# Attention of a two-layer trunk: a pair's preparation in shorter VectorE steps, 1/rms from ScalarE's ln and exp with one Newton step, and transposes issued later

## The chip, the cores and the metric

The kernel runs as one program on one core of a Trainium2 chip. The metric is device time in microseconds (us), from runs of the whole program. The core's engines are TensorE (PE in the profile; PEld is its loading of weights), VectorE (DVE), ScalarE (ACT), GpSimd (POOL) and SyncE (SP, which issues DMAs). Each engine takes its own instructions in the order in which they were placed, and waits where an operand is not ready.

## The reference, cut to what matters

Two layers process 128 context tokens (the prompt) and 1024 latent tokens. Each layer projects its input, runs three groups of heads (attention, a short convolution, retention), joins them by `w_o`, and follows with a dense SwiGLU block. Attention has 8 heads; a query and a key have 96 numbers, of which the last 32 carry a rotary position code (rope). Both are divided by their own root mean square (rms) before the scores are made:

```python
q = (_rmsnorm(q_lat, q_norm_g) @ w_q_up).reshape(b, t, MLA_HEADS, QK_HEAD)
q = _rmsnorm(q, q_head_g)
k, v = _mla_kv(c_kv, k_pe, w_kv_up, k_head_g)
if latent:
    q = jnp.concatenate([q[..., :QK_NOPE], _rope_2d(q[..., QK_NOPE:])], axis=-1)
    k = jnp.concatenate([k[..., :QK_NOPE], _rope_2d(k[..., QK_NOPE:])], axis=-1)
    k_c, v_c = _mla_kv(ctx_ckv, ctx_kpe, w_kv_up, k_head_g)
    k = jnp.concatenate([k, k_c], axis=1)
    v = jnp.concatenate([v, v_c], axis=1)
attn = _attention(q.transpose(0, 2, 1, 3), k.transpose(0, 2, 1, 3), v.transpose(0, 2, 1, 3))
```

`_rmsnorm` is `x * rsqrt(mean(x * x) + EPS)`, and `_attention` a softmax of `q k / sqrt(96)` times `v`. The latent queries meet 1024 latent and 128 cached context keys, 9 key tiles of 128. The prompt's 128 tokens attend only to themselves.

## The kernel before

A layer runs in four stages: `in_proj` (projections of the layer's input, with the convolution, retention and the first pair's preparation placed between them), `attention`, the output projection, and the SwiGLU block. The change touches `in_proj` in one number, and `attention`. Products that must be exact to float32 are split in a high and a low part, so one product is three matmuls.

`attention(l, R, x)` works on 8 heads in 4 pairs. It is written as Python generators whose `yield`s mark where work may be broken off:

- `head_main` (the main work of one head): for each of 9 key tiles, three matmuls for each half of the 1024 queries (lines 1127 to 1129) into one of three PSUM tiles called mm, ScalarE's exponential of each (line 1130), and the product of the tile before with v (line 1110, tile ax, 64 rows of output). GpSimd adds the exponentials up over key tiles (lines 1113 and 1119), since their sum divides the result at the end.
- `head_prep` (through `heads`; one head ahead): transposes of the pair's k and q (line 1070), copies to high and low parts (ScalarE, line 1073; VectorE, line 1074), then 24 products for the scores' row maxima (line 1081), each reduced by VectorE (line 1083). The last reduction and a sign change give `mn` (lines 1087, 1088), which TensorE transposes (line 1090) and VectorE spreads over 8 extra rows of q (line 1092), so that the main products come out with the maximum subtracted.
- `pair_prep` (through `pairs`; one pair ahead): 10 token tiles, each with 9 matmuls (lines 960 to 969) or 3 for the last, ScalarE's copies and sums of squares (`ssq`, lines 971 to 981), one `yield` per tile. Then VectorE's chain: three operations on `ssq`, `rsq` for 1/rms (line 233: a bit trick in two operations, and three Newton steps of three operations each, lines 239 to 241, in tiles `rsy` and `rst`), and per half of the tokens `rope` (lines 918 to 921, products `rp`) and the products of q and k with 1/rms (lines 995, 997, 998).
- `pairs` then lets `GAP` (5) yields pass, marks the pair ready, and runs `prompt`: the prompt's own small attention of that pair (lines 1016 to 1050). After the last pair it loads and splits parts of the next stage's input (`mix_load`).

`attention` runs `head_main` of head h, and after each of its yields advances the other two by credit: `acc[0]` gains `RA` (1.3) for `heads`, whose yields carry prices (`CT`, `CM`, `CB`), and `acc[1]` gains `RB` (0.7) for `pairs`, one step per whole unit. What is left of the heads' credit goes to the pairs at `RX`. `LEAD` says from which yield on the next head may be prepared. A scheduler then orders the instructions of each engine by this order and their dependencies. All small products (transposes, maxima, projections, the products with v) share five PSUM tiles called `ax`. The first pair's `pair_prep` runs inside `in_proj`, advanced by `step(3)` after each column block.

## Time and profile before

| what | value |
|---|---|
| median of 3 runs | 3169.8 us (3165.72 to 3171.39) |
| profiled execution, its own time | 3169.16 us |
| its span, first to last instruction | 3167.4 us |
| mean granted TensorE clock | 0.977 of full speed |
| busy share of TensorE, VectorE, ScalarE, GpSimd | 96%, 56%, 35%, 37% |

The profiled execution is one run with the hardware profiler on. Its span leaves out what lies before the first and behind the last instruction. The busy shares are means over all four stages of both layers; attention, which the change touches, takes the stretch from about 380 to 700 us in layer 0 and from about 1943 to 2263 us in layer 1, a fifth of the span together. A window's row gives the busy time of each engine in it, with the count of instructions in brackets, and the granted clock in shares of the full one.

### The profile page before, as it was taken

The numbers are of one execution on the slowest core, as the hardware profiler recorded it, in microseconds if no ns is written. First come the engines' busy times: TensorE is split into PE (matmuls) and PEld (weight loads), VectorE is DVE, ScalarE is ACT, GpSimd is POOL, SyncE is SP. The second block draws the span as 40 slices with busy tenths as digits, with TensorE's granted clock in tenths as the row PEclk, the third lists the DMA queues.
The fourth block names the chain that finished last, engine by engine and source line by source line (L and its number), as shares of the span: only waits on it lengthen the run. The fifth ranks groups of instructions, "written<-read, shape, count | busy, mean of one in ns | idle before, by whom it ended". The sixth has DMA issues, their size and how long they took to land.

```text
span 3167.4 us, 48782 instructions
## 1 busy us (share of the span) xinstructions
PE 3033.0 (96%) x19136; PEld 2686.3 (85%) x19136; DVE 1778.7 (56%) x3483; ACT 1113.2 (35%) x2646; POOL 1178.4 (37%) x764
## 2 busy tenths in 40 slices
PE   6999999999799999999999999899988999999999
PEld 5988855459799999998999896554788999999999
DVE  6264476766954555633272646767588455556343
ACT  4333455444522222321153235454444222223211
POOL 3111243465643443411242103434656434343212
PEclk8999998999899999999999999999998999999999
DMA  5323000123222122576231110010322222226323
GB/s 211 103 95 128 22 12 1 60 91 107 83 81 74 63 84 81 178 251 237 66 113 48 49 32 13 12 53 8 121 100 69 84 84 71 69 71 220 101 67 100
DMA packets 126726, 278.06 MB, mean 88 GB/s; under 512 B 24097, under 2 KB 47393, under 8 KB 126497
## 3 DMA queue, kind: packets, MB, share of 16 engines
q1 hardware_dynamic: 126496, 274.95, 25.8%
q8 instruction: 151, 2.47, 0.3%
q14 instruction: 79, 0.64, 0.1%
HBM read 222.57 MB, written 52.33 MB: 87 GB/s over the span
## 4 chain that ended last, share of the span: by engine, by line
PE 81%; DVE 12%; DMA 2%; ACT 2%; issue 2%; POOL 1%; SPq 0%; DVEq 0%; POOLq 0%; ACTq 0%
PE mm L227 14%; PE mm L229 14%; PE mm L228 14%; PE ax L227 6%; PE ax L229 6%; PE ax L228 6%; PE ax L1110 5%; PE ax L1081 2%; PE mm L1127 2%; PE mm L1129 2%; PE mm L1128 1%; PE ax L325 1%; PE ax L1070 1%; DVE mx L1083 1%; POOL W L213 1%
## 5 line engine op out<-in xcount | busy, mean ns | idle before, releaser
L213 POOL TENSOR_TENSOR W<-r,W 128x512 fp32r<-128x512 f32 x336 | 447.8, 1346 | 541.7 <-ACT W L212 530.7
L213 POOL TENSOR_TENSOR W<-W,W 128x640 fp32r<-128x640 f32 (+5 forms) x168 | 298.4, 1777 | 827.9 <-ACT W L212 477.1
L227 PE MATMUL mm<-gh,W 128*128 128x384 f32 x1056 | 354.8, 336 | 1.9 <-DVE u L1401 1.1
L229 PE MATMUL mm<-gh,W 128*128 128x384 f32 x1056 | 353.3, 335 | 0.9 <-POOL W L213 0.8
L228 PE MATMUL mm<-gl,W 128*128 128x384 f32 x1056 | 352.9, 334 | 0.0
L1246 DVE SCALAR_TENSOR_TENSOR x<-mm,mod,x 128x128 f32<-128x128 f32 (+2 forms) x320 | 157.9, 515 | 329.7 <-PE mm L229 327.6
L229 PE MATMUL ax<-hth,W 128*128 128x288 f32 x1056 | 314.6, 298 | 10.1 <-POOL W L213 10.1
L227 PE MATMUL ax<-hth,W 128*128 128x288 f32 x1056 | 314.8, 298 | 7.6 <-ACT W L212 7.6
L228 PE MATMUL ax<-htl,W 128*128 128x288 f32 x1056 | 314.1, 298 | 0.0
L1119 POOL TENSOR_TENSOR W<-W,W 128x1024 f32<-128x1024 f32 x96 | 230.8, 2404 | 222.2 <-ACT W L1130 220.6
L212 ACT CAST W<-r 128x512 fp32r<-128x512 f32 x336 | 205.2, 621 | 184.8 <-DMA r<-in_w_up 63.8
L212 ACT CAST W<-W 128x640 fp32r<-128x640 f32 (+5 forms) x168 | 131.5, 783 | 390.6 <-DMA W<-in_w_down 178.7
L1083 DVE TENSOR_REDUCE mx<-ax 128x1 f32<-128x384 f32 x384 | 195.7, 550 | 115.2 <-PE ax L1081 112.8
L1130 ACT ACTIVATE W<-mm 128x512 f32<-128x512 f32 x288 | 168.5, 605 | 218.1 <-PE mm L1129 210.6
L227 PE MATMUL mm<-hh,W 128*128 128x384 f32 x704 | 240.5, 342 | 0.0
L229 PE MATMUL mm<-hh,W 128*128 128x384 f32 x704 | 239.0, 339 | 0.0
L228 PE MATMUL mm<-hl,W 128*128 128x384 f32 x704 | 237.9, 338 | 0.0
L1110 PE MATMUL ax<-W,vt 128*64 128x512 f32 x576 | 208.4, 658 | 8.2 <-DVE attn L1162 6.7
L229 PEld LDWEIGHTS ax<-hth,W 128*128 128x128 f32 x1056 | 201.2, 191 | 11.3 <-POOL W L213 11.3
L227 PEld LDWEIGHTS mm<-gh,W 128*128 128x128 f32 x1056 | 198.2, 188 | 13.0 <-issue 9.9
L227 PEld LDWEIGHTS ax<-hth,W 128*128 128x128 f32 x1056 | 201.4, 191 | 8.5 <-ACT W L212 8.5
L228 PEld LDWEIGHTS ax<-htl,W 128*128 128x128 f32 x1056 | 201.3, 191 | 0.0
(333 smaller groups left out, 7864.7 us busy)
## 6 DMA issues: line engine op xcount, KB each, us to landing
W<-in_ada_w SPq DMA_DIRECT2D x80, 512.0 KB, 5.1
gr<-gd SPq DMA_DIRECT2D x44, 576.0 KB, 5.4
r<-in_w_gate SPq DMA_DIRECT2D x96, 256.0 KB, 2.8
r<-in_w_up SPq DMA_DIRECT2D x96, 256.0 KB, 4.2
W<-in_w_in_fm SPq DMA_DIRECT2D x30, 512.0 KB, 3.7
W<-in_w_down SPq DMA_DIRECT2D x48, 320.0 KB, 3.5
gd<-gu SPq DMA_DIRECT2D x22, 576.0 KB, 3.7
gd<-gu SPq DMA_DIRECT2D x44, 224.0 KB, 2.2
```

The costliest lines, as they stand in the source:

```text
L212: self.nc.scalar.copy(hi, raw)
L213: self.nc.gpsimd.tensor_tensor(lo, raw, hi.bitcast(F32), op=ALU.subtract)
L227: self.nc.tensor.matmul(ps, wh, xh, start=first and i == 0, stop=False)
L228: self.nc.tensor.matmul(ps, wh, xl, start=False, stop=False)
L229: self.nc.tensor.matmul(ps, wl, xh, start=False, stop=last and i == n - 1)
L1081: nc.tensor.matmul(ps, qh[0:96, qt * P:(qt + 1) * P], kh[0:96, c * CH:(c + 1) * CH], start=True, stop=True)
L1083: nc.vector.reduce_max(mx[:, qt, c:c + 1], ps, axis=AX.X)
L1110: nc.tensor.matmul(po[64 * qc:64 * qc + 64, :], vv[:, kt, b:b + 64], prs[kt][:, qs], start=(kt == 0), stop=(kt == 8))
L1119: nc.gpsimd.tensor_tensor(acc, acc, prs[kt], op=ALU.add)
L1127: nc.tensor.matmul(ps, kh[0:104, ks], qh[0:104, qs], start=True, stop=False)
L1130: nc.scalar.activation(pr[:, qs], ps, AF.Exp, scale=SCALE)
L1246: self.nc.vector.scalar_tensor_tensor(x[m][:, t0:t1], ps[:, t0 - c * CH:t1 - c * CH], self.mod[l][:, j, m, i:i + 1], x[m][:, t0:t1], ALU.m ...
```

## The change

1. `1/rms`: `rsq` is replaced by ScalarE's `Ln` and `Exp` (with scale -0.5) and one Newton step of three VectorE operations.
2. `rope_steps` is `rope` with a yield behind each two operations, and further yields stand in VectorE's chain. `RB` rises from 0.7 to 1.0, and `GAP` with its five yields becomes two.
3. In `prompt`, the scaling of q, k, the maxima and the probabilities goes from VectorE to ScalarE, and the product with `gq` to GpSimd. Three yields are added.
4. In `head_prep` the reduction for `mn` gives the negated maximum itself, and a second yield of price `CB` stands between it and the transpose.
5. In `in_proj`, from the tenth column block on the background work advances by four steps instead of three.

```diff
@@ -48,7 +48,7 @@
 
 
 CT, CM, CB, RX = 0.7, 1.4, 0.7, 0.5
-RA, RB, LEAD, GAP = 1.3, 0.7, 14, 5
+RA, RB, LEAD = 1.3, 1.0, 14
 
 
 def segs(c):
@@ -780,7 +780,7 @@
                 else:
                     nc.scalar.copy(dst[:, cs], ps)
                 self.tick(ticks)
-                step(3)
+                step(4 if i > 8 else 3)
             if kind == "rq":
                 rq.append(dst)
             elif kind == "gc":
@@ -919,6 +919,18 @@
         nc.vector.tensor_tensor(t2, x, tab[:, 1].unsqueeze(2).to_broadcast(sh), op=ALU.mult)
         nc.vector.tensor_tensor(out[:, :, :, 0:16], t1[:, :, :, 0:16], t2[:, :, :, 16:32], op=ALU.subtract)
         nc.vector.tensor_tensor(out[:, :, :, 16:32], t2[:, :, :, 0:16], t1[:, :, :, 16:32], op=ALU.add)
+
+    def rope_steps(self, x, tab):
+
+        V = self.nc.vector
+        sh = [P, 4, x.shape[2], 32]
+        t1, t2 = self.Tt("rp1", sh), self.Tt("rp2", sh)
+        V.tensor_tensor(t1, x, tab[:, 0].unsqueeze(2).to_broadcast(sh), op=ALU.mult)
+        V.tensor_tensor(t2, x, tab[:, 1].unsqueeze(2).to_broadcast(sh), op=ALU.mult)
+        yield
+        V.tensor_tensor(x[:, :, :, 0:16], t1[:, :, :, 0:16], t2[:, :, :, 16:32], op=ALU.subtract)
+        V.tensor_tensor(x[:, :, :, 16:32], t2[:, :, :, 0:16], t1[:, :, :, 16:32], op=ALU.add)
+        yield
 
     def pair_weights(self, l, p, R):
         if ("w", p) not in R:
@@ -980,21 +992,31 @@
             for j in range(2):
                 nc.scalar.activation(sq[:, j, 0:64], kvp[:, j * 64:(j + 1) * 64], AF.Square, accum_out=ssq[:, 2 + j, t:t + 1])
             yield
-        V = nc.vector
+        V, G = nc.vector, nc.gpsimd
         V.tensor_tensor(ssq[:, 2:4, :], ssq[:, 2:4, :], R["kvs2"].unsqueeze(1).to_broadcast([P, 2, 10]), op=ALU.mult)
         V.tensor_tensor(ssq[:, 2:4, :], ssq[:, 2:4, :], R["kpss"].unsqueeze(1).to_broadcast([P, 2, 10]), op=ALU.add)
+        yield
         V.tensor_scalar(ssq[:, 2:4, :], ssq[:, 2:4, :], 1.0 / 96, EPS, ALU.mult, ALU.add)
         V.scalar_tensor_tensor(ssq[:, 0:2, 0:9], ssq[:, 0:2, 0:9], 1.0 / 96,
                                R["qms"].unsqueeze(1).to_broadcast([P, 2, 9]), ALU.mult, ALU.add)
-        r = self.rsq(ssq, (P, 4, 10))
+        r, t = self.sm("rsy", (P, 4, 10)), self.sm("rst", (P, 4, 10))
+        nc.scalar.activation(r, ssq, AF.Ln)
+        nc.scalar.activation(r, r, AF.Exp, scale=-0.5)
+        yield
+
+        V.tensor_tensor(t, r, r, op=ALU.mult)
+        V.scalar_tensor_tensor(t, t, -0.5, ssq, ALU.mult, ALU.mult)
+        yield
+        V.scalar_tensor_tensor(r, t, 1.5, r, ALU.add, ALU.mult)
         yield
         for b in range(2):
-            self.rope(q[b][:, :, :, 64:96], R["rtab"][:, :, 4 * b:4 * b + 4])
+            yield from self.rope_steps(q[b][:, :, :, 64:96], R["rtab"][:, :, 4 * b:4 * b + 4])
             t0, n = 1 + 4 * b, 4 + b
             bc = lambda i, n, m: r[:, i:i + 2, t0:t0 + n].rearrange("p a b -> p b a").unsqueeze(3).to_broadcast([P, n, 2, m])
             V.tensor_tensor(q[b], q[b], bc(0, 4, 96), op=ALU.mult)
             yield
             V.tensor_tensor(k[b][:, :, :, 0:64], k[b][:, :, :, 0:64], bc(2, n, 64), op=ALU.mult)
+            yield
             V.tensor_tensor(k[b][:, :, :, 64:96],
                             R["kper"][:, t0:t0 + n, :].unsqueeze(2).to_broadcast([P, n, 2, 32]), bc(2, n, 32), op=ALU.mult)
             yield
@@ -1013,10 +1035,13 @@
         at = self.attn_tile(p, R)
         gains = self.gains(l)
         for hh in range(2):
-            V.tensor_tensor(pr[:, hh, 64:96], pr[:, hh, 64:96], R["gq"], op=ALU.mult)
-            V.tensor_scalar(pr[:, hh, :], pr[:, hh, :], r[:, hh, 0:1], None, ALU.mult)
-            V.tensor_scalar(pr[:, 2 + hh, 0:64], pr[:, 2 + hh, 0:64], r[:, 2 + hh, 0:1], None, ALU.mult)
-            V.tensor_scalar(pr[:, 2 + hh, 64:96], R["kper"][:, 0, :], r[:, 2 + hh, 0:1], None, ALU.mult)
+            nc.gpsimd.tensor_tensor(pr[:, hh, 64:96], pr[:, hh, 64:96], R["gq"], op=ALU.mult)
+            nc.scalar.mul(pr[:, 2 + hh, 0:64], pr[:, 2 + hh, 0:64], r[:, 2 + hh, 0:1])
+            nc.scalar.mul(pr[:, 2 + hh, 64:96], R["kper"][:, 0, :], r[:, 2 + hh, 0:1])
+        yield
+        for hh in range(2):
+            nc.scalar.mul(pr[:, hh, :], pr[:, hh, :], r[:, hh, 0:1])
+        yield
         pt = self.ax((96, 4, P))
         for i in range(4):
             nc.tensor.transpose(pt[:, i, :], pr[:, i, :], self.ident)
@@ -1029,14 +1054,15 @@
             nc.tensor.matmul(ps[:, hh, :], qk[:, hh, :], qk[:, 2 + hh, :], start=True, stop=True)
         m, den = self.sm("pm", (P, 2)), self.sm("pden", (P, 2))
         V.reduce_max(m, ps, axis=AX.X)
-        V.tensor_scalar(m, m, -SCALE, None, ALU.mult)
+        nc.scalar.mul(m, m, -SCALE)
         pp = self.Tt("pp", (P, 2, P))
         for hh in range(2):
             nc.scalar.activation(pp[:, hh, :], ps[:, hh, :], AF.Exp, scale=SCALE, bias=m[:, hh:hh + 1],
                                  accum_out=den[:, hh:hh + 1])
         V.reciprocal(den, den)
         for hh in range(2):
-            V.tensor_scalar(pp[:, hh, :], pp[:, hh, :], den[:, hh:hh + 1], None, ALU.mult)
+            nc.scalar.mul(pp[:, hh, :], pp[:, hh, :], den[:, hh:hh + 1])
+        yield
         yield
         pt = self.ax((P, 2, P))
         for hh in range(2):
@@ -1082,10 +1108,10 @@
                                  start=True, stop=True)
                 nc.vector.reduce_max(mx[:, qt, c:c + 1], ps, axis=AX.X)
                 yield CM / 3
+        mn = self.sm("mn", (P, 8))
+        nc.vector.tensor_reduce(mn, mx, axis=AX.X, op=ALU.max, negate=True)
         yield CB
-        mn = self.sm("mn", (P, 8))
-        nc.vector.reduce_max(mn, mx, axis=AX.X)
-        nc.vector.tensor_scalar(mn, mn, -1.0, None, ALU.mult)
+        yield CB
         pt = self.ax((8, P))
         nc.tensor.transpose(pt, mn, self.ident)
         o, _ = VEC["eye8"]
@@ -1181,10 +1207,9 @@
                 yield from self.pair_prep(l, p, R)
                 if p < 3:
                     self.pair_weights(l, p + 1, R)
-                for _ in range(GAP):
-                    yield
+                yield
+                yield
                 R["ready", p] = True
-                yield
                 yield from self.prompt(l, p, R)
             while self.head_lim < 7:
                 yield
```

The places where the order changes most lie around pairs 1 and 2 of layer 0. On VectorE, at the end of head 3's maxima, the rows before read as follows (`mx` are the maxima by block, `mn` the negated row maximum, `rp` the rope products, `qt` and `kt` the pair's q and k, `rsy` 1/rms, `W` the head's q with its 8 extra rows):

```order
L1083 TENSOR_REDUCE mx_4293<-ax_4489 128x1
L918 TENSOR_TENSOR rp_787_4492<-qt_3990,rtabq_2373 128x256
L919 TENSOR_TENSOR rp_788_4493<-qt_3990,rtabq_2373 128x256
L1087 TENSOR_REDUCE mn_4502<-mx_4293 128x8
L997 TENSOR_TENSOR kt_3992<-kt_3992,rsy_4409 128x10x64
L920 TENSOR_TENSOR qt_3990<-rp_787_4492,rp_788_4493 128x8x16
L921 TENSOR_TENSOR qt_3990<-rp_788_4493,rp_787_4492 128x8x16
L1088 TENSOR_SCALAR mn_4502<-mn_4502 128x8
L998 TENSOR_TENSOR kt_3992<-kper_2354,rsy_4409 128x10x32
L995 TENSOR_TENSOR qt_3990<-qt_3990,rsy_4409 128x768
L1092 TENSOR_TENSOR W_4181<-ax_4505,vec_95 8x1024
```

In the changed kernel the same place reads:

```order
L1109 TENSOR_REDUCE mx_4327<-ax_4471 128x1
L928 TENSOR_TENSOR rp_788_4476<-qt_3976,rtabq_2373 128x256
L1112 TENSOR_REDUCE mn_4474<-mx_4327 128x8
L929 TENSOR_TENSOR rp_789_4477<-qt_3976,rtabq_2373 128x256
L1018 TENSOR_TENSOR kt_3978<-kt_3978,rsy_4339 128x10x64
L1118 TENSOR_TENSOR W_4224<-ax_4491,vec_95 8x1024
L931 TENSOR_TENSOR qt_3976<-rp_788_4476,rp_789_4477 128x8x16
L932 TENSOR_TENSOR qt_3976<-rp_789_4477,rp_788_4476 128x8x16
L1020 TENSOR_TENSOR kt_3978<-kper_2354,rsy_4339 128x10x32
L1016 TENSOR_TENSOR qt_3976<-qt_3976,rsy_4339 128x768
```

The sign change of line 1088 is gone, `mn`'s reduction has moved ahead of one rope product, and its use (the product on 8 partitions, line 1092 before and 1118 after) stands ahead of the rest of the rope. The last product on `kt` still follows behind four more operations.

On TensorE, the last projection of pair 1 (`cch` and `ccl` are the cached context's latents, `kTh` and `kTl` the head's k, `vt` its v) stands before in this order; from its last row there are 30 rows to the first transpose of that pair's k:

```order
L1127 MATMUL mm_3716<-W_2784,kTh_2782 128x512
L1128 MATMUL mm_3716<-W_2785,kTh_2782 128x512
L1129 MATMUL mm_3716<-W_2784,kTl_2783 128x512
L967 MATMUL ax_3721<-qwh_3325,cch_2343 128x256
L968 MATMUL ax_3721<-qwl_3326,cch_2343 128x256
L969 MATMUL ax_3721<-qwh_3325,ccl_2344 128x256
L1110 MATMUL ax_3329<-W_3654,vt_2421 64x512 x2
```

In the changed kernel it stands between a head's maxima (line 1107), and 48 rows lie between its last row and the first transpose of the pair's k:

```order
L1107 MATMUL ax_3668<-kTh_3335,W_3337 128x384
L1136 MATMUL ax_3322<-W_3586,vt_2421 64x512
L979 MATMUL ax_3671<-qwh_3318,cch_2343 128x256
L980 MATMUL ax_3671<-qwl_3319,cch_2343 128x256
L981 MATMUL ax_3671<-qwh_3318,ccl_2344 128x256
L1136 MATMUL ax_3322<-W_3586,vt_2421 64x512
L1107 MATMUL ax_3683<-kTh_3335,W_3337 128x384
```

The projection has moved ahead against the main work of the head, and the transposes have kept their place.

On ScalarE, behind the last sums of squares of pair 1 (`sqj`, `ssq`), the order before is (line 1130 are the exponentials):

```order
L981 ACTIVATE sqj_3727,ssq_3387<-ax_3721 128x64 x2
L1130 ACTIVATE W_3750<-mm_3751 128x512
L1130 ACTIVATE W_3750<-mm_3756 128x512
L1130 ACTIVATE W_3788<-mm_3789 128x512
L1130 ACTIVATE W_3788<-mm_3794 128x512
L1157 ACTIVATE dy_3802<-ax_3799 128x512
```

In the changed kernel the logarithm, the exponential for 1/rms and the scalings stand among those exponentials:

```order
L993 ACTIVATE sqj_3677,ssq_3358<-ax_3671 128x64 x2
L1156 ACTIVATE W_3694<-mm_3695 128x512
L1156 ACTIVATE W_3694<-mm_3700 128x512
L1003 ACTIVATE rsy_3709<-ssq_3358 128x40
L1004 ACTIVATE rsy_3709<-rsy_3709 128x40
L1156 ACTIVATE W_3721<-mm_3722 128x512
L1156 ACTIVATE W_3721<-mm_3727 128x512
L1039 ACTIVATE qt_3353<-qt_3353,rsy_3709 128x64
L1040 ACTIVATE qt_3353<-kper_2354,rsy_3709 128x32
L1039 ACTIVATE qt_3353<-qt_3353,rsy_3709 128x64
L1040 ACTIVATE qt_3353<-kper_2354,rsy_3709 128x32
```

Two exponentials stand between `Exp` of line 1004 and the first scaling of line 1039. Line 1003 needs VectorE's work on `ssq`, and line 1039 VectorE's Newton step.

## Rows read from the trace of the kernel before

**Rows 1.** The page: its first line, and busy time of each engine.

```profile
span 3167.4 us, 48782 instructions
...
PE 3033.0 (96%) x19136; PEld 2686.3 (85%) x19136; DVE 1778.7 (56%) x3483; ACT 1113.2 (35%) x2646; POOL 1178.4 (37%) x764
```

**Rows 2.** Windows of layer 0's attention: us, busy of PE, PEld, DVE, ACT, POOL, PEclk, DMA, GB/s.

```profile
380.00:700.00 320.00, 296.16 (x1261) 166.84 (x1260) 228.80 (x398) 160.34 (x502) 152.71 (x76) 0.95 0.10 37
```

**Rows 3.** The same view, seven short windows of that stage.

```profile
404.00:414.00 10.00, 5.95 (x22) 3.51 (x21) 9.95 (x12) 3.12 (x5) 6.88 (x4) 0.72 0.01 2
454.00:463.00 9.00, 6.70 (x31) 5.14 (x30) 6.89 (x9) 3.70 (x16) 2.37 (x1) 0.81 0.17 67
472.00:480.00 8.00, 6.23 (x17) 2.64 (x16) 8.00 (x21) 1.19 (x2) 4.14 (x2) 0.79 0.00 1
486.00:497.00 11.00, 7.30 (x27) 3.18 (x23) 9.04 (x10) 3.24 (x6) 7.13 (x5) 0.69 0.00 0
505.00:518.00 13.00, 10.63 (x31) 4.42 (x30) 10.29 (x16) 3.62 (x11) 6.38 (x3) 0.74 0.00 0
557.00:566.00 9.00, 5.58 (x19) 2.42 (x18) 8.85 (x12) 1.79 (x3) 4.71 (x3) 0.81 0.28 87
640.00:651.00 11.00, 7.75 (x19) 2.79 (x20) 9.76 (x15) 2.30 (x6) 5.28 (x3) 0.84 0.00 0
```

**Rows 4.** The same view, the last of these places in layer 1.

```profile
2203.00:2218.00 15.00, 11.76 (x23) 4.13 (x24) 11.19 (x18) 2.23 (x6) 6.10 (x3) 0.66 0.00 1
```

**Rows 5.** Order of time on DVE, 394 to 409: start us, us, operation, [idle before].

```profile
394.57 1.61 DVE L984 TENSOR_TENSOR ssq<-ssq,kvs 128x20 f32<-128x20 f32 x1 [1.46 <-ACT sqj L981]
...
397.89 0.28 DVE L921 TENSOR_TENSOR qt<-rp,rp 128x128 f32<-128x128 f32 x1
...
406.27 2.62 DVE L998 TENSOR_TENSOR kt<-kper,rsy 128x320 f32<-128x320 f32 x1
```

**Rows 6.** Order of time on DVE and POOL, 472 to 492.

```profile
472.45 1.91 DVE L237 TENSOR_SCALAR rsy<-rsy 128x40 int32<-128x40 int32 x1
...
484.00 2.92 DVE L997 TENSOR_TENSOR kt<-kt,rsy 128x640 f32<-128x640 f32 x1
...
488.30 2.39 POOL L1119 TENSOR_TENSOR W<-W,W 128x1024 f32<-128x1024 f32 x1
...
488.41 2.42 DVE L921 TENSOR_TENSOR qt<-rp,rp 128x128 f32<-128x128 f32 x1
...
490.76 1.07 DVE L1088 TENSOR_SCALAR mn<-mn 128x8 f32<-128x8 f32 x1
```

**Rows 7.** Order of time on DVE, 556 to 562.

```profile
556.94 2.40 DVE L240 SCALAR_TENSOR_TENSOR rst<-rst,ssq 128x40 f32<-128x40 f32 x1
...
560.08 1.80 DVE L241 SCALAR_TENSOR_TENSOR rsy<-rst,rsy 128x40 f32<-128x40 f32 x1
```

**Rows 8.** Order of time on DVE, 572 to 575.

```profile
572.31 2.66 DVE L998 TENSOR_TENSOR kt<-kper,rsy 128x320 f32<-128x320 f32 x1
```

**Rows 9.** Windows of tile rst: us, DVE busy (x), PEclk, DMA, GB/s.

```profile
380.00:700.00 320.00, 10.71 (x27) 0.95 0.10 37
```

**Rows 10.** Groups of line and form, 380 to 700: busy, mean ns | idle before.

```profile
L1088 DVE TENSOR_SCALAR mn<-mn 128x8 f32<-128x8 f32 x7 | 4.7, 673 | 0.2
...
L1019 DVE TENSOR_SCALAR qt<-kper,rsy 128x32 f32<-128x32 f32 x6 | 3.6, 594 | 0.0
...
L1017 DVE TENSOR_SCALAR qt<-qt,rsy 128x96 f32<-128x96 f32 x6 | 3.1, 509 | 0.0
...
L1032 DVE TENSOR_SCALAR pm<-pm 128x2 f32<-128x2 f32 x3 | 2.8, 925 | 0.0
...
L237 DVE TENSOR_SCALAR rsy<-rsy 128x40 int32<-128x40 int32 x3 | 2.2, 750 | 0.0
...
L1035 ACT ACTIVATE pp<-ax,pm 128x128 f32<-128x128 f32 x6 | 2.1, 362 | 4.1 <-DVE pm L1032 4.1
```

**Rows 11.** Waits of ACT, 380 to 700: us in total, times, longest us.

```profile
ACT pp L1035 <- DVE pm L1032: 4.1, 3, 2.9
```

## Prediction

> **What bounds the kernel now.** I read the page first: the span, the busy shares and the sliced busy digits. TensorE is busy 96% of the span [rows 1], so only the few stretches where it waits, or runs at half clock, can give time back; every engine that the change touches is far from full. The second view is the windows of the attention stage, where the edited code runs: of 320 us in layer 0, TensorE is busy 296.2, VectorE 228.8, ScalarE 160.3, GpSimd 152.7, and the granted clock is 0.95 [rows 2]. So 24 us are idle there, and more is lost to the clock. Layer 1 repeats the stage about 1563 us later.
>
> The third view is the same table cut around the seven places with idle of over 1.7 us [rows 3]. I call them A (404 to 414), B (454 to 463), C (472 to 480), D (486 to 497), E (505 to 518), F (557 to 566) and G (640 to 651). The idle is the width minus TensorE's busy time; the clock's loss I take as width times (1 minus the granted clock), an upper bound, since some of the slow clock falls into the idle itself. Each place is followed by a drop of the clock from 2.4 to 1.2 GHz. Idle plus clock: A 4.05 + 2.80, B 2.30 + 1.71, C 1.77 + 1.68, D 3.70 + 3.41, E 2.37 + 3.38, F 3.42 + 1.71, G 3.25 + 1.76; 37.3 us. In layer 1 they repeat; only G costs clearly more there, 3.24 + 5.10 [rows 4]. I take 37 us a layer for the rest of the working.
>
> What ends these waits is VectorE, which is busy 9.95 of the 10 us at A and all 8 at C [rows 3], although each of its operations there is small. Why it is late is seen in the order of time. The rope difference of line 921 takes 0.28 us at 397.89 [rows 5] and 2.42 us at 488.41; a GpSimd sum started at 488.30 and ended at 490.69, and the VectorE operation ended with it [rows 6]. Operations on PSUM, such as the maxima of line 1083, don't show this. Two or three such blocked operations in a row make a wait at TensorE: at C line 237 is 1.91 us long; at D lines 997 and 921 stand between the reduction for mn and its sign change (line 1088), which ends at 491.83, and TensorE's transpose waits for that [rows 6]. At F two of the Newton operations (2.40 and 1.80 us) stand ahead of the two attn products that release PSUM [rows 7]. A single blocked one does no harm: line 998 takes 2.66 us at 572.31 [rows 8], and no window with idle lies there, because five PSUM tiles are in flight.
>
> One page says the same and something that speaks against the change. The Trainium skill (SBUF — State Buffer, section Who interferes with whom) states that a VectorE instruction with two SBUF inputs contends with a GpSimd instruction that reads SBUF, and the loser waits for the whole instruction, while TensorE and ScalarE wait for nobody. The trace agrees (line 921: 0.28 against 2.42 us). By that rule what goes to ScalarE is free of the wait, but the two-input operations that stay are exposed as before, and spreading them out gives each its own chance to meet a GpSimd sum. What that would cost is the second rival below.
>
> **What the change removes.** Per pair eight of the eleven VectorE operations for 1/rms, the eight scalings and gain products of the prompt's q and k, the scaling of the prompt's maxima and of its probabilities; per head the sign change of line 1088. Over pairs 1 to 3 of a layer: Newton operations 10.7 us for 27 [rows 9], of which two thirds, 7.1 us; line 237 2.2, line 1017 3.1, line 1019 3.6, line 1032 2.8, line 1088 4.7 [rows 10]: 23.5 us, and some small ones not shown. That is a tenth of VectorE's busy time, and more than half of it is blocked time. It counts only at the places.
>
> **What it adds.** On ScalarE eleven small operations a pair; the nearest row, an exponential of 128 columns, takes 0.36 us [rows 10], so at most 4 us a pair or 12 us a layer on an engine that is idle for half of the stage. On GpSimd two products of 32 columns a pair, small beside sums of 2.4 us [rows 6]. More important, ScalarE now waits twice a pair for VectorE (ln for the sums of squares, the first scaling for the finished Newton step), and behind it in its queue stand the exponentials that empty TensorE's three mm tiles.
>
> **What it moves.** A pair's projections advance one step per half key tile instead of 0.7. In the order of TensorE pair 1's last projection is followed by 48 rows, not 30, before the first transposes of its k. At the stage's mean of 296.2 us for 1261 matmuls [rows 2], 0.235 us each, that is 4.2 us more lead (estimate). The reduction for mn now gives the sign itself, and a second short yield stands ahead of its transpose.
>
> **Place by place, in each layer.**
> - A, worth 6.9. VectorE's chain for pair 1 runs from 394.57 to 408.89, 14.3 us [rows 5]. It starts 4.2 earlier and loses (10.71 x 2/3 + 2.2) / 3 = 3.1 us of 1/rms operations, but takes in head 1's mn (0.7, the mean of line 1088 [rows 10]), the product on 8 partitions behind it, one more rope product, and ln and exp on ScalarE (0.36 each [rows 10]): some 3 us, with two estimates of 0.8 for the products. It ends about 4.3 us earlier, and the idle is 4.05. I take 5.
> - C, worth 3.5: line 237 is gone and the rest stands singly between maxima. I take 2.5.
> - D, worth 7.1: mn no longer waits behind lines 997, 920 and 921, but k's last product still stands behind all of them and the 8x1024 product, and the transposes of k come right after mn's; most of the wait moves there. I take 2.5. The bounds are 0 and 7.1.
> - E, worth 5.8: line 1032 and the two products on pp leave, the blocked reciprocal step stays. I take 3.
> - F, worth 5.1: the Newton operations are gone from between the attn products. I take 4.
> - B, worth 4.0, gets two rope products and one small operation on two inputs: some 1.0 us alone, up to 2.4 more if blocked. I take 1.5 as a loss.
> - G is the splitting of mix tiles, untouched.
> - ScalarE's new waits: bounds 0 and, per wait, the 2.9 us of the longest wait of ScalarE for VectorE now [rows 11]. TensorE has three mm tiles of cover. I take 1 us a pair, 3 a layer.
>
> 17 - 1.5 - 3 = 12.5 us a layer, 25 for both. In in_proj, pair 0's work is issued faster (four steps instead of three from the tenth weight on) and lies beside dense projections; I cost it at nothing, since a stall of a microsecond or two there is the most that so small a shift makes. The profiled execution took 3169.16 us, 1.8 more than its span and 0.6 less than the median of the runs, so 3169.2 - 25 = **3144 us**.
>
> **The rivals.**
> 1. Nearly everything goes: the five places A, C to F are worth 28.3 us a layer, less B's 1.5: 54 us, 3115. For it speaks that VectorE is the only releaser; against it, that D's chain keeps its length.
> 2. The waits form again: GpSimd is busy 0.48 of the stage [rows 2], so an isolated two-input operation meets a sum of 2.4 us about every second time and waits 1.2 us. Blocks that now come in a row come one by one, but twelve of them a pair leave room for two close ones. If one such pair of blocks costs what C costs now, 3.5 us, six pairs lose 21 of the 25 us: 3165, no change that can be told. The row at 572.31 speaks against it, the full windows of A and C for it.
> 3. ScalarE's queue, slower: the sums of squares or the Newton step are late by one or two blocks, ln or the scaling holds the exponentials, the three mm tiles run full and TensorE stops. If both waits cost 2.9 us, and each brings F's clock loss of 1.7, a pair loses 9.2, six lose 55, against 31 us gained without any: 24 us slower, 3193. It decides from 31 / 6 = 5.2 us a pair on. For it speaks that ScalarE already waits 4.1 us for VectorE in three times [rows 11]; against it, that between ln and the scaling two exponentials are placed, and that the three tiles hold some 2 us of TensorE's work.
>
> **How the numbers follow.** Forecast (3126 to 3155): 0.55. Rival 1 (under 3126): 0.08. Rival 2 and what lies between (3155 to 3176): 0.23, of which 0.10 is still below 3163.5. Rival 3 (over 3176): 0.14. About 0.2% (6.3 us) is what a measurement of this kernel tells from no change, so faster is under 3163.5: 0.73; within 0.13; slower 0.14. The range, 3116 to 3172, reaches to rival 1 and over rival 2; the forecast's own is 3126 to 3155.
>
> **What would show it.** At A the wait of the transposes for line 998's successor gone or under 1.5 us; no wait of mn's transpose behind k's product at D, but one of the transposes; F under 1 us; VectorE some 20 us less busy in the stage; the granted clock there up from 0.95 to about 0.97; G unchanged. It is wrong if TensorE waits for the exponentials, with ScalarE waiting for ssq or rsy for over 2 us at a time, or if the maxima are waited for at new places as long as at C.

## The result, and the profile after

The changed kernel takes 3117.94 us (median of 4 runs, 3115.68 to 3125.01), the kernel before 3169.74 us. The ratio is 0.9845, with a 95% interval of 0.9828 to 0.9863: 51.8 us faster. That is inside the stated range and on the forecast side, but it is twice the forecast gain of 25 us: the forecast's own band, 3126 to 3155, is missed, and the time lies where the first rival ("nearly everything goes", 3115) put it.

The page of the changed kernel, first line and busy times (to compare with [rows 1]):

```profile
span 3113.8 us, 48728 instructions
...
PE 3016.3 (97%) x19136; PEld 2678.3 (86%) x19136; DVE 1708.1 (55%) x3315; ACT 1131.7 (36%) x2734; POOL 1185.4 (38%) x780
```

The span is 53.6 us shorter. VectorE has 168 instructions fewer and 70.6 us less to do, ScalarE 88 more and 18.5 us more, which hardly move their shares.

To compare the stage I take it from its first main matmul to its last product with v. Before, it runs from 357.1 to 693.1 us in layer 0 and takes 335.9 us (338.5 in layer 1); after, from 353.7 to 665.9, 312.2 us (312.7). So 23.7 and 25.8 us of the 53.6 are gained in the two attention stages. The stretch up to layer 0's attention became 3.4 us shorter, but it varies from 351.7 to 357.2 over all traces of this study, among kernels that share its code too, so it is no effect that can be told.

The windows of the changed kernel's attention in layer 0, and of three short places in it (us, busy of PE, PEld, DVE, ACT, POOL, PEclk, DMA share, GB/s; to compare with [rows 2, 3]):

```profile
353.70:665.90 312.20, 304.84 (x1338) 173.59 (x1337) 206.67 (x352) 181.06 (x597) 160.00 (x83) 0.99 0.11 38
477.00:483.00 6.00, 4.83 (x28) 2.72 (x28) 5.97 (x8) 2.58 (x6) 3.97 (x4) 1.00 0.00 0
523.00:530.00 7.00, 5.32 (x27) 2.72 (x26) 6.26 (x12) 5.41 (x15) 2.63 (x3) 1.00 0.00 0
612.00:620.00 8.00, 4.34 (x12) 1.05 (x8) 7.97 (x10) 2.15 (x6) 4.36 (x2) 0.92 0.00 0
```

TensorE is idle for 7.4 of the 312.2 us, and the granted clock is 0.99 (0.95 before). The waits of TensorE in this stretch, all of them (engine, tile and line, releaser: us in total, times, longest):

```profile
PE ax L1107 <- DVE mx L1109: 3.6, 1, 3.6
PE ax L1096 <- DVE kTl L1100: 1.5, 1, 1.5
PE ax L1096 <- DVE kt L1020: 1.2, 1, 1.2
PE ax L1179 <- DVE W L1143: 0.5, 1, 0.5
PE ax L1179 <- POOL W L1143: 0.4, 1, 0.4
PE ax L1107 <- ACT W L1099: 0.2, 1, 0.2
```

Before, seven places had idle of over 1.7 us [rows 3]. One of them is left: the first row, which is G. The waits of A, B, C, E and F have no successor. D's has one, the third row: the transposes of k wait 1.2 us for k's last product (477 to 483), and the clock stays at 1.00 there. The second row is new, 1.5 us at 523 to 530, where VectorE's operations on the next pair, one of them held for 2.35 us at 521.91, stand ahead of the low parts of k (line 1100) that the transposes of q wait for; the clock stays full there too.

At A, the chain of pair 1, in order of time on DVE and POOL:

```profile
387.75 0.17 DVE L996 TENSOR_TENSOR ssq<-ssq,kvs 128x20 f32<-128x20 f32 x1
...
390.56 0.92 DVE L1007 TENSOR_TENSOR rst<-rsy 128x40 f32<-128x40 f32 x1
...
392.02 2.64 POOL L1145 TENSOR_TENSOR W<-W,W 128x1024 f32<-128x1024 f32 x1
...
392.36 3.12 DVE L1016 TENSOR_TENSOR qt<-qt,rsy 128x768 f32<-128x768 f32 x1
...
400.05 0.48 DVE L1020 TENSOR_TENSOR kt<-kper,rsy 128x320 f32<-128x320 f32 x1
```

It starts at 387.75, 34.1 us after the stage's start (394.57, 37.5 us, before [rows 5]), and ends at 400.53, 46.8 us after it (51.8 before). Three of its operations are still held by GpSimd sums: line 1007 takes 0.92 us, line 1016 takes 3.12, and line 1018 behind it 1.77 at 395.41. But TensorE does not reach the transposes of k until 404.81, so nobody waits.

At D, on DVE:

```profile
473.56 0.17 DVE L1112 TENSOR_REDUCE mn<-mx 128x8 f32<-128x24 f32 x1
...
477.24 1.35 DVE L932 TENSOR_TENSOR qt<-rp,rp 128x128 f32<-128x128 f32 x1
...
478.52 1.83 DVE L1020 TENSOR_TENSOR kt<-kper,rsy 128x320 f32<-128x320 f32 x1
```

`mn` is reduced at 473.6, ahead of the rope; two blocked operations (1.35 and 1.83 us) still stand ahead of k's transposes, where three did before (lines 997, 920 and 921 [rows 6]).

G, on DVE and POOL, is as it was: four splitting operations of `mix_split` take 6.1 us beside two GpSimd sums, and the maxima behind them come 3.6 us late. The first row is that of the kernel before.

```profile
639.17 5.76 DVE L1230 TENSOR_TENSOR mh<-mr,mh 128x288 fp32r<-128x288 f32 x4
...
611.04 6.08 DVE L1255 TENSOR_TENSOR mh<-mr,mh 128x288 fp32r<-128x288 f32 x4
...
611.45 4.99 POOL L1145 TENSOR_TENSOR W<-W,W 128x1024 f32<-128x1024 f32 x2
...
617.15 2.88 DVE L1109 TENSOR_REDUCE mx<-ax 128x1 f32<-128x384 f32 x6
```

The new waits of ScalarE for VectorE, which the third rival rested on (`ssq` before ln, `rsy` before the first scaling; to compare with [rows 11]):

```profile
ACT rsy L1003 <- DVE ssq L999: 3.0, 2, 2.7
...
ACT qt L1039 <- DVE rsy L1010: 0.8, 1, 0.8
```

They are there, three waits of 3.8 us in all, but TensorE waits for no exponential: the only wait for ScalarE among its rows above is 0.2 us long.

### The profile page after: what moved, and what is told of

Read it like the earlier page. It is cut to its first block, busy times and chain, and to the rows that moved or that the text cites. A ratio compares the mean times of both kernels' runs of the same rounds, so it can differ in the third digit from the quotient of the medians.

```text
span 3113.8 us, 48728 instructions
## 1 busy us (share of the span) xinstructions
PE 3016.3 (97%) x19136; PEld 2678.3 (86%) x19136; DVE 1708.1 (55%) x3315; ACT 1131.7 (36%) x2734; POOL 1185.4 (38%) x780
## 4 chain that ended last, share of the span: by engine, by line
PE 85%; DVE 9%; ACT 2%; DMA 2%; issue 1%; POOL 1%; SPq 0%; DVEq 0%; POOLq 0%; ACTq 0%
PE mm L227 14%; PE mm L229 14%; PE mm L228 14%; PE ax L227 6%; PE ax L228 6%; PE ax L229 6%; PE ax L1136 5%; PE ax L1107 3%; PE mm L1153 2%; PE mm L1154 2%; PE mm L1155 2%; PE ax L325 1%; PE ax L1096 1%; DVE hb L1389 1%; DVE hy L1411 1%
## 5 line engine op out<-in xcount | busy, mean ns | idle before, releaser
L229 PE MATMUL mm<-hh,W 128*128 128x384 f32 x704 | 238.6, 339 | 0.0
```

Of the source, the lines that this page charges most:

```text
L229: self.nc.tensor.matmul(ps, wl, xh, start=False, stop=last and i == n - 1)
```

## Experiments

A figure used below is VectorE's **blocked time**: over all its instructions in the two attention stages, the duration minus the shortest duration of the same line and form in the same trace, summed. It is 120.5 us before and 70.4 after. It counts whatever makes an operation longer: 19 to 25 us are left of it where GpSimd's sums are left out (e3 and e4 below).

| kernel | median us | ratio to before (95%) | attention, layer 0 / 1, us | blocked time, us |
|---|---|---|---|---|
| before | 3169.7 | 1 | 335.9 / 338.5 | 120.5 |
| after | 3117.9 | 0.9845 (0.9828 to 0.9863) | 312.2 / 312.7 | 70.4 |
| e1_order | 3150.8 | 0.9950 (0.9938 to 0.9962) | 327.9 / 330.0 | 104.6 |
| e2_ops | 3128.4 | 0.9878 (0.9865 to 0.9891) | 316.8 / 318.0 | 82.4 |
| e3_nosum_before | 3086.6 | 0.9754 (0.9739 to 0.9769) | 298.2 / 298.2 | 24.8 |
| e4_nosum_after | 3091.6 | 0.9759 (0.9744 to 0.9774) | 300.4 / 300.5 | 18.9 |
| e5_half_before | 3152.1 | 0.9957 (0.9942 to 0.9972) | 328.6 / 328.2 | 95.9 |
| e7_rsq_only | 3163.7 | 0.9986 (0.9976 to 0.9996) | 335.7 / 332.0 | 107.4 |
| e8_prompt_only | 3148.7 | 0.9933 (0.9921 to 0.9946) | 321.1 / 326.4 | 96.6 |
| e9_mn_only | 3161.1 | 0.9978 (0.9968 to 0.9987) | 333.0 / 330.8 | 106.7 |
| e10_share_after | 3127.8 | 0.9870 (0.9854 to 0.9887) | 318.1 / 319.1 | 76.5 |
| e11_rate_only | 3192.1 | 1.0069 (1.0056 to 1.0083) | 344.8 / 348.9 | 91.6 |
| e12_after_rsq_undone | 3135.9 | 0.9895 (0.9878 to 0.9913) | 322.7 / 319.3 | 84.8 |
| e13_after_prompt_undone | 3130.2 | 0.9879 (0.9864 to 0.9894) | 318.4 / 319.3 | 86.7 |

The kernels ran on several chips, each beside runs of the kernel before on its own chip, whose medians lie between 3167.9 and 3169.7; kernels are best compared by their ratios.

**What makes VectorE late: GpSimd's sums.** My theory was that VectorE's operations that get held until a GpSimd sum ends make TensorE wait; the rival, that VectorE simply has too much to do at those places. Two edits of the kernel before leave VectorE's work alone. e3_nosum_before leaves most of the sums out:

```diff
             if kt == 1:
-                nc.gpsimd.tensor_tensor(acc, prs[0], prs[1], op=ALU.add)
+                nc.gpsimd.memset(acc, 1.0)
...
-            elif kt > 1:
-                nc.gpsimd.tensor_tensor(acc, acc, prs[kt], op=ALU.add)
```

> The kernel before, with GpSimd's running sums of the exponentials left out for all but the last key tile (the denominators are not the reference's). If GpSimd's sums make VectorE late: TensorE's idle in attention falls from 24 to under 10 us a layer and the time to 3115 to 3130, as low as the changed kernel or lower. If VectorE is late by its own operations: 3160 to 3172.

3086.6, lower than any theory had said: 81 us, with the same 416 VectorE instructions as the kernel before in the stage. Windows of its attention in layer 0:

```profile
357.20:655.40 298.20, 295.95 (x1338) 171.79 (x1337) 187.99 (x416) 174.46 (x564) 31.09 (x31) 1.00 0.11 40
```

TensorE is busy 295.95 of the 298.2 us and the clock stands at 1.00. A VectorE with only its own work is in time everywhere, G included. So the rival falls. Leaving the sums out does one thing more: a sum holds the exponentials' buffers until it has read them, so without it ScalarE, and TensorE behind it, could go on sooner. The rows of the kernel before leave little room for that: ScalarE waits once in the stage for a sum,

```profile
ACT W L1130 <- POOL W L1119: 2.8, 1, 2.8
```

and TensorE waits there for the exponentials 0.5 us in all, which stay in e3_nosum_before. e5_half_before keeps every sum and cuts it in two:

```diff
-                nc.gpsimd.tensor_tensor(acc, acc, prs[kt], op=ALU.add)
+                for s in (slice(0, 512), slice(512, 1024)):
+                    nc.gpsimd.tensor_tensor(acc[:, s], acc[:, s], prs[kt][:, s], op=ALU.add)
```

> The kernel before, with each running sum of GpSimd (128x1024) as two instructions of 512 columns. If VectorE waits for the end of the GpSimd instruction that is running, its longest waits halve to about 1.3 us and the excess over undisturbed durations in attention falls from 120 us towards 60; the idle of TensorE falls with it: 3140 to 3155. If VectorE is late by the number of its operations alone, or by the share of time that GpSimd is busy whatever the size of an instruction: 3164 to 3176.

3152.1. The group of these sums (line, engine, forms and count | busy, mean ns | idle before):

```profile
L1121 POOL TENSOR_TENSOR W<-W,W 128x512 f32<-128x512 f32 x96 | 126.6, 1339 | 93.3 <-ACT W L1132 93.3
```

GpSimd is busy longer (171.7 us in the stage against 158.4), but a sum's instruction is 1.34 us long instead of 2.39 [rows 6], and the time falls by 0.43%. So GpSimd's busy share does not set the time; the length of the instruction that VectorE meets counts. The blocked time fell to 95.9, not to 60, since more sums are met: 98 VectorE operations of the two stages are held by over 0.2 us, 74 before.

e4_nosum_after is the changed kernel with the sums left out in the same way:

> The changed kernel, with GpSimd's running sums of the exponentials left out for all but the last key tile (the denominators are not the reference's). e3_nosum_before took 3086.6. If all that the change gains is gained from VectorE's waits for GpSimd, the two come out alike: 3081 to 3091. If the change also gains by less work or an earlier start: 3070 to 3080. If ScalarE's waits for VectorE, or the longer queue on ScalarE, cost something that the gain covers: 3092 to 3105.

3091.6, between the first band and the third (from 3092, ScalarE's waits or its queue cost something); its ratio, 0.9759, and that of e3_nosum_before, 0.9754, lie inside each other's intervals. Its stage in layer 0:

```profile
351.70:652.10 300.40, 299.97 (x1338) 172.43 (x1336) 177.52 (x352) 181.44 (x597) 31.92 (x36) 1.00 0.11 40
```

Without GpSimd's sums the change gains nothing, although VectorE does 10.5 us less in the stage (177.5 against 188.0). TensorE is nearly full in both kernels, so no wait is left that less work or an earlier start could shorten: the 51.8 us are waits that do not arise without GpSimd's sums, and their consequences. If anything the change costs a little here: each stage is some 2.2 us longer than in e3_nosum_before, with 4.0 us more of TensorE's busy time for the same 1338 matmuls at the same clock. No run shows why.

**Operations or order.** e1_order has the changed kernel's yields, `RB`, the second `CB` and step 4 with the operations of before; e2_ops the reverse.

e1_order, against the changed kernel (the three Newton steps and the other scalings go back likewise):

```diff
-        nc.scalar.activation(r, ssq, AF.Ln)
-        nc.scalar.activation(r, r, AF.Exp, scale=-0.5)
+        V.tensor_scalar(yi, ssq.bitcast(mybir.dt.int32), 1, None, ALU.logical_shift_right)
+        V.tensor_scalar(yi, yi, -1, MAGIC, ALU.mult, ALU.add)
         yield
...
-            nc.scalar.mul(pr[:, hh, :], pr[:, hh, :], r[:, hh, 0:1])
+            V.tensor_scalar(pr[:, hh, :], pr[:, hh, :], r[:, hh, 0:1], None, ALU.mult)
...
-        nc.vector.tensor_reduce(mn, mx, axis=AX.X, op=ALU.max, negate=True)
+        nc.vector.reduce_max(mn, mx, axis=AX.X)
+        nc.vector.tensor_scalar(mn, mn, -1.0, None, ALU.mult)
```

e2_ops, against the changed kernel:

```diff
-RA, RB, LEAD = 1.3, 1.0, 14
+RA, RB, LEAD, GAP = 1.3, 0.7, 14, 5
...
-            yield from self.rope_steps(q[b][:, :, :, 64:96], R["rtab"][:, :, 4 * b:4 * b + 4])
+            self.rope(q[b][:, :, :, 64:96], R["rtab"][:, :, 4 * b:4 * b + 4])
```

> The changed kernel's order and pacing (yields between VectorE's steps, RB 1.0, two yields instead of GAP, the second CB, step 4) with the operations of before: the bit trick and three Newton steps on VectorE, cut by yields, the prompt's scalings on VectorE, the sign change of mn as an operation of its own. Theory P (it is the order that takes VectorE's blocks off the places where TensorE waits): 3120 to 3135, attention 314 to 320 us a layer. Theory O (it is the smaller number of VectorE operations open to a wait for GpSimd): 3150 to 3165, attention 330 us or more a layer. If both matter alike: about 3143.

> The changed kernel's operations (ln and exp with one Newton step, the prompt's scalings on ScalarE and GpSimd, the negating reduction) with the order of before: no new yields, RB 0.7, GAP 5, one CB, step 3. Theory P: 3150 to 3165, with the waits at C, D and E back and little left of A and F. Theory O: 3118 to 3130. If both matter alike: about 3143.

e1_order took 3150.8 and e2_ops 3128.4: both as theory O says, if barely (the attention of e1_order, 327.9 and 330.0, is at the edge of the 330 or more that it named). The operations alone give 1.22%, some 39 us; the order adds 0.33% to them, some 10.5 us (0.9878 against 0.9845), and gives 0.5% with the old operations. In e2_ops the waits at B (second row), C and G (in the first) stand, and ScalarE waits longer for VectorE than in the changed kernel (its TensorE and ScalarE rows):

```profile
PE ax L1100 <- DVE mx L1102: 6.9, 4, 3.2
PE ax L1100 <- DVE W L1093: 1.6, 2, 1.4
...
ACT rsy L1002 <- DVE ssq L998: 5.6, 3, 3.2
...
ACT qt L1035 <- DVE rsy L1007: 4.0, 2, 2.7
```

Even these 9.6 us over three pairs reach TensorE nowhere: no exponential is in the list of its waits.

The places, in layer 0, divide between the two. B and C are gone in e1_order and stand in e2_ops; A, E and F are gone in e2_ops, where D keeps 0.8 us; in e1_order D keeps 2.7, E 0.7 and F 1.1 us. At C the operations alone did not help: line 237 is gone from e2_ops, but the last operation of its Newton step is held in its stead, beside a sum that starts at 461.97, and the idle there is 2.4 us (1.8 before):

```profile
462.15 2.35 DVE L1007 SCALAR_TENSOR_TENSOR rsy<-rst,rsy 128x40 f32<-128x40 f32 x1
```

**The operations one by one,** each alone in the kernel before, but for one thing: all three also place the prompt's scalings of q behind those of k, as the changed kernel does, which no run separates. e7_rsq_only:

```diff
-        r = self.rsq(ssq, (P, 4, 10))
+        r, t = self.sm("rsy", (P, 4, 10)), self.sm("rst", (P, 4, 10))
+        nc.scalar.activation(r, ssq, AF.Ln)
+        nc.scalar.activation(r, r, AF.Exp, scale=-0.5)
+        V.tensor_tensor(t, r, r, op=ALU.mult)
+        V.scalar_tensor_tensor(t, t, -0.5, ssq, ALU.mult, ALU.mult)
+        V.scalar_tensor_tensor(r, t, 1.5, r, ALU.add, ALU.mult)
```

e8_prompt_only, where the other scalings and that of the maxima by -SCALE move likewise, and the gain product to GpSimd:

```diff
-            V.tensor_scalar(pr[:, hh, :], pr[:, hh, :], r[:, hh, 0:1], None, ALU.mult)
+            nc.scalar.mul(pr[:, hh, :], pr[:, hh, :], r[:, hh, 0:1])
```

e9_mn_only:

```diff
-        nc.vector.reduce_max(mn, mx, axis=AX.X)
-        nc.vector.tensor_scalar(mn, mn, -1.0, None, ALU.mult)
+        nc.vector.tensor_reduce(mn, mx, axis=AX.X, op=ALU.max, negate=True)
```

> The kernel before with one part of the change alone: 1/rms from ScalarE's ln and exp with one Newton step; order and the rest as before. e2_ops gained 39.5 us with three such parts. If the gain of a part goes with the blocked time of the VectorE operations that it removes (the Newton operations and line 237 make up 23.5 - 14.2 = 9.3 of the 23.5 us of the prediction's list): about 0.4 of 39.5, 3148 to 3158, with C and F gone and A shorter. If ScalarE's queue behind ln holds TensorE up: 3165 or more, with waits of ScalarE for ssq of over 2 us.

> The kernel before with one part of the change alone: the prompt's scalings, the scaling of its maxima and of its probabilities on ScalarE, the gain product on GpSimd. If the gain goes with the blocked time removed (lines 1017, 1019 and 1032: 9.5 of 23.5 us): about 0.4 of 39.5, 3148 to 3158, with E shorter and the second wait at A (line 1022) gone. If these operations lie off the path: 3163 to 3172.

> The kernel before with one part of the change alone: the reduction for mn negates itself, and line 1088 is gone. If the gain goes with the blocked time removed (4.7 of 23.5 us): about 0.2 of 39.5, 3158 to 3164, with D shorter since mn's transpose no longer waits behind lines 997 and 921. If D's wait moves to the transposes of k: 3164 to 3172.

e8_prompt_only (3148.7, 0.67%) and e9_mn_only (3161.1, 0.22%) came as their first bands say, though in e9_mn_only part of D's wait moved to the transposes of k, as its second band has it (2.4 us there, 3.7 before). e7_rsq_only did not: 3163.7, a gain of 0.14% where 10 to 20 us were expected. TensorE's waits in layer 0 show why:

```profile
PE ax L1109 <- DVE mn L1107: 4.9, 2, 4.3
PE ax L1041 <- DVE qt L1038: 4.7, 1, 4.7
PE ax L1129 <- DVE mx L1102: 3.4, 1, 3.4
```

The wait at F and that of k's transposes at A are gone, as expected, but at A the prompt's transposes now wait 4.7 us, and those at D and E became longer (4.3 for mn's transpose, 3.4 for maxima); C, expected gone, has 2.4 us as in e2_ops. On POOL and DVE at A:

```profile
403.59 2.73 POOL L1132 TENSOR_TENSOR W<-W,W 128x1024 f32<-128x1024 f32 x1
...
404.04 2.32 DVE L1036 TENSOR_SCALAR qt<-kper,rsy 128x32 f32<-128x32 f32 x1
...
406.40 2.34 POOL L1138 TENSOR_TENSOR W<-W,W 128x1024 f32<-128x1024 f32 x1
...
407.67 1.12 DVE L1035 TENSOR_SCALAR qt<-qt,rsy 128x64 f32<-128x64 f32 x1
...
408.86 0.44 DVE L1038 TENSOR_SCALAR qt<-qt,rsy 128x96 f32<-128x96 f32 x2
```

k's chain ended before the sum of 403.59; now the prompt's scalings meet it, and the next one at 406.40. One wait went, others came. In layer 1 the wait of 4.7 us came too, but D's there is only 0.8. In e8_prompt_only the reverse is seen; what is left of its list in layer 0 are the waits at C and G (first row), F and B, and of A's 2.8 us 0.5:

```profile
PE ax L1094 <- DVE mx L1096: 5.6, 3, 3.2
...
PE ax L1123 <- DVE attn L1175: 3.4, 1, 3.4
...
PE ax L1094 <- DVE W L1087: 1.4, 1, 1.4
...
PE ax L1083 <- DVE kt L1010: 0.5, 1, 0.5
```

D's 3.7 us are gone there too, though none of D's operations was changed. In layer 1 of the same execution they are not (mn's transpose waits; the view names the product on k that ended beside mn's sign change):

```profile
PE ax L1103 <- DVE kt L1010: 3.9, 1, 3.9
```

There three held operations, of 2.61, 2.10 and 2.42 us, stand ahead of the sign change; in layer 0 the same three take 0.41, 0.81 and 0.28. So the blocks in a row of lines 997, 920 and 921 [rows 6] are a coincidence of that chain with GpSimd's operations, which a shift of a few microseconds undoes or brings back. Of the 5.3 us between this kernel's two attention stages 3.4 are idle, about that one wait.

**Parts of the order and of the operations, in the changed kernel.** e11_rate_only is the kernel before with `RB` 1.0 and two yields for `GAP`'s five. e12_after_rsq_undone and e13_after_prompt_undone are the changed kernel with one group of operations taken back, with the edits of e1_order.

> The kernel before with RB 1.0 and two yields in place of GAP's five and the one behind: the pair's preparation is advanced faster, its blocks of VectorE work stay uncut. e1_order gained 17 us with this, the cut steps, the second CB and step 4. If the earlier start is what the order brings: 3145 to 3157. If the cutting of the blocks is: 3162 to 3175, since whole blocks only move to other places.

> The changed kernel with 1/rms by the bit trick and three Newton steps on VectorE again, cut by three yields; everything else as changed. Alone, the ln and exp gave only 4.4 us, because the waits moved to the prompt's transposes and to mn's. If they add to the rest no more than that: 3118 to 3126. If they are worth their share once the prompt's scalings are off VectorE: 3128 to 3140.

> The changed kernel with the prompt's scalings on VectorE again (its yields stay); everything else as changed. Alone they gave 19.4 us. If that is worth the same here: 3133 to 3142. If it is worth more because the five yields of GAP no longer lie between the chain and the prompt (the rate alone made the prompt's transposes wait 5.0 to 6.9 us for line 1017 at each pair): 3145 to 3160. If the cut steps cover it: 3118 to 3128.

e11_rate_only took 3192.1, slower than the kernel before by 0.69% and outside both bands:

```profile
PE ax L1022 <- DVE qt L1017: 17.0, 3, 6.9
```

With the blocks of the preparation uncut and `GAP`'s yields gone, the prompt's transposes wait at all three pairs, 17 us in layer 0. Between this kernel and e1_order lie the cut steps (the prompt's too), the second `CB` and step 4; together they are worth some 38 us (1.19% by the ratios). The earlier start alone is not what the order brings.

e12_after_rsq_undone took 3135.9. In the changed kernel the ln and exp are thus worth 0.50% (0.9895 against 0.9845), over three times what they gave alone. Its new waits of TensorE:

```profile
PE ax L1181 <- DVE W L1145: 2.3, 1, 2.3
...
PE mm L1155 <- DVE W L1120: 1.8, 1, 1.8
...
PE ax L1109 <- DVE attn L1190: 1.1, 1, 1.1
```

e13_after_prompt_undone took 3130.2, between two bands: the prompt's scalings are worth 0.34% here, half of what they gave alone. The parts don't add: what one part frees is lent to whichever chain is late next.

**A step further.** e10_share_after puts half of every sum's columns on VectorE:

```diff
-                nc.gpsimd.tensor_tensor(acc, acc, prs[kt], op=ALU.add)
+                for s, eng in ((slice(0, 512), nc.gpsimd), (slice(512, 1024), nc.vector)):
+                    eng.tensor_tensor(acc[:, s], acc[:, s], prs[kt][:, s], op=ALU.add)
```

> The changed kernel, with columns 512 to 1023 of every running sum on VectorE and the others on GpSimd, so that GpSimd's instructions are half as long and no more than before. VectorE gets some 0.68 us for each, 33 us more a layer on the 204 to 209 that it is busy now. If the waits for GpSimd are what is left: 3098 to 3110. If VectorE's own load then makes TensorE wait: 3118 to 3140.

3127.8, 0.25% slower than the changed kernel. VectorE's half (group, busy and mean ns):

```profile
L1143 DVE TENSOR_TENSOR W<-W,W 128x512 f32<-128x512 f32 x56 | 57.9, 1035 | 17.9 <-ACT W L1154 16.5
```

An undisturbed one takes 0.68 us, this mean is 1035 ns: of the 56 in layer 0, 25 take over 0.75 us, 22 of them beside a half sum on GpSimd that had started just before. G's wait shrank to 1.5 us, but waits of up to 1.9 us came at other places. The time lies in the second band, that of VectorE's own load, which grew by 33.7 us in the stage; how much of the loss is load and how much the meeting of the halves, the run does not separate. No kernel with the reference's output was faster than the changed one.

## Why the prediction was right, and where its sizes were off

**The bound and the mechanism** held. VectorE's holds by GpSimd sums are what TensorE waited for; e3, e4 and e5 show it by taking the sums away and by cutting them, and in e4 nothing of the change's gain is left. The Trainium skill (SBUF — State Buffer, section Who interferes with whom) says that the engine that comes second waits for the whole instruction of the other; the trace agrees, with holds up to the length of a sum, and with the 15.7 us that e5 gained with sums of 1.34 us in place of 2.39. The warning that I took from it, that spread two-input operations each meet their own sum, is true of single operations. At A (lines 1007, 1016 and 1018) it cost nothing, because the chain ended before TensorE came to its transposes; at 523 to 530 one such operation is behind the new wait of 1.5 us.

That the time lies in the stated range is owed to the range's width: it ends at 3116, 2 us below the measured time, and the region under 3126 had been given a chance of 0.08.

**Place by place, in layer 0.** A (5 of 6.9), C (2.5 of 3.5) and F (4 of 5.1) went wholly; C not for the reason given first, the loss of line 237, but for the second, the spreading between maxima (e1_order and e2_ops). Three terms were mis-sized. **D**: I took 2.5 of 7.1, on the ground that most of the wait moves to k's transposes; it does move there, but 1.2 us of it, and without the clock's drop. **E**: 3 of 5.8, on the ground that the blocked reciprocal step stays; the whole of E went. **B**: a loss of 1.5 was taken, a gain of 4.0 came. The operation that is blocked at both is line 1160, the last step of the reciprocal of the heads' denominators (line 1186 in the changed kernel; the prompt's own reciprocal, line 1037, was never blocked, 0.16 us in the mean). At B and at E, first before, then after:

```profile
454.65 2.72 DVE L1160 SCALAR_TENSOR_TENSOR dy<-dt,dy 128x512 f32<-128x512 f32 x1
...
508.37 2.58 DVE L1160 SCALAR_TENSOR_TENSOR dy<-dt,dy 128x512 f32<-128x512 f32 x1
...
446.95 0.69 DVE L1186 SCALAR_TENSOR_TENSOR dy<-dt,dy 128x512 f32<-128x512 f32 x1
...
487.59 0.68 DVE L1186 SCALAR_TENSOR_TENSOR dy<-dt,dy 128x512 f32<-128x512 f32 x1
```

It is the same operation, and it stayed; what went is its meeting with a sum. In layer 0 of e1, e2, e7, e8, e9, e12 and e13 B's wait stands exactly where this step takes 2.72 us (e2, e7, e8, e9), and E's exactly where it takes 2.6 (e7); elsewhere the step takes 0.68 us and at most 0.7 us of idle is left. The fault behind all three terms is one: I kept a wait where an operation that had been blocked stayed in the chain, as if the block belonged to the operation. e8_prompt_only shows the same of D, gone in one layer and there in the other with its operations untouched.

**ScalarE's new waits** were taken at 3 us a layer. They are in the trace (3.8 us over three pairs), at TensorE they cost nothing that its waits show. The third rival's point of 5.2 us a pair was not neared; e2_ops, with 9.6 us over three pairs, did not feel it either.

**What all that was worth** is less than the places' sum. With the true outcomes the 37.3 us of the seven places lose 31.1 (all of A, B, C, E and F, 25.2; 5.9 of D's 7.1), and the new wait takes back 1.5. The stage gained 23.7. Idle fell by 16.5 (23.8 to 7.4). The other 7.2 are a fall of TensorE's busy time, which I put down to the clock; the bound, time at the lower level counted half, says 15.4 (34.1 us at that level before, 3.4 after). The prediction had called that an upper bound, and used it as the size. Nor are the 7.2 surely the clock's alone: e3 and e4, both at 1.00 throughout, differ by 4.0 us of busy time. By the idle and 0.47 of the bound (7.2 / 15.4), and with all but G gone, the sum would have been 17.6 + 6.9 = 24.5 us a layer and the time 3120; the 0.47 is taken from the result, so this shows where the forecast went off, and not that it could have been made. So the outcome of the places was taken too small by more than the clock was taken too large.

**The second rival**, that waits form again, did not decide here, yet e7_rsq_only and e11_rate_only show it at work: in these the gain of an edit is lost at the next chain. That the change escapes it is due to its parts together. The runs say which part removed which place (B and C go with the order, F with ln and exp), but which coincidence of chain and sum a part removes depends on a few microseconds, and I have no account of it from which the parts' values could have been worked out beforehand; this stays open. So does G: of the kernels that keep the sums, only e10_share_after made it clearly shorter, at a price elsewhere.

**The signs to look for** came out right: `mn`'s transpose waits no longer, k's do a little; F is under 1 us; VectorE is 32 us less busy in the stage (238.6 to 206.7 in layer 0) where 20 were named; the clock is 0.99 where 0.97 was; G is unchanged.

## What to carry to other kernels

Where VectorE shares its time with long GpSimd instructions, price its operations by the holds and not by their own durations: take the GpSimd work out once, though the output is then another, and the time saved (here 81 us) estimates what rearranging can bring. A wait that three holds in a row make belongs to no single operation; small edits move it, so values of parts measured one at a time need not add, and a part that gives little alone (0.14%) can be worth 0.50% once its neighbours are gone. Speeding up a background chain without cutting it, or without the slack behind it, can be worse than leaving it.

## What the runs showed of the hardware

A GpSimd memset holds VectorE too. In the kernel before, on POOL:

```profile
490.75 1.05 POOL L1076 MEMSET kTh<- 8x1152 f32 x1
```

Line 1088, a product of 128x8 with one input, started at 490.76 and ended at 491.83 [rows 6], with this memset; undisturbed it takes 0.17 us. In layer 1 of e8_prompt_only the same operation ends 0.03 us behind that memset, too.

In an attention stage with hardly any idle of TensorE (2.25 us in e3_nosum_before, 0.43 in e4_nosum_after) the granted clock stays at 1.00 throughout. So the waits that went gave back more than themselves: 7.2 us of TensorE's busy time beside 16.5 of idle in layer 0, and 9.5 beside 16.3 in layer 1 (25.8 gained, idle from 23.6 to 7.3). The waits of 1.2 and 1.5 us that are left in the changed kernel's layer 0 were not followed by a drop of the clock (1.00 in both windows); G's 3.6 us were (0.92).
